# The first 8 MB of a ReLU row sum: even 64 KB stretches in one half of the partitions, odd ones in the other

## The chip, the core and the metric

The kernel runs on one NeuronCore of one Trainium2 chip. The metric is the device time of one execution in microseconds (us). The time before is the median of 3 runs.

## What is computed

The input has 32 x 512 rows of 1024 float32 values, 64 MB in all. Each row is clamped at zero and summed, which leaves one float32 for a row.

```python
batch, seq, dim = 32, 512, 1024
...
def reference(x):
    relu_x = np.maximum(x, 0)
    return np.sum(relu_x, axis=-1).astype(np.float32)
```

## The kernel before

The 16384 rows are seen as 128 partitions of 128 rows. A row of the input is 4 KB, and 16 rows, one column group of a buffer in one partition, are a contiguous 64 KB stretch.

**Two views of memory.** The first 2048 rows (8 MB, `N1`) have a view of their own, `xf`: partition p holds rows 16 p to 16 p + 15, so the 128 stretches of 64 KB lie one behind the other in memory and go to partitions 0, 1, 2 and so on. The remaining 14336 rows are `xv`: partition p holds 112 consecutive rows, and a load takes the same 16 of each partition, so its 64 KB stretches are 448 KB apart. The output has the same two views, `of` and `ov`. `rows(m, n)` and `sums(m, n)` pick the view: below 16 (`ROWS`) the first one.

**Loads.** There are three SBUF buffers `io0` to `io2`, each of 128 x 16 x 1024 float32 (8 MB). All DMAs are issued by SyncE (SP), in program order. Seven loads of 8 MB go round the three buffers (the loop over `j`); they are called load 0 to load 6 here. Load 0 alone takes its rows from `xf`. It is moved ahead of the opening of the program by `open_without_barrier`. Loads 1 and 2 follow with no wait. From load 3 on, a load waits on a semaphore that DVE raises when it has summed the buffer's old content. The last 16 rows of each partition come in six smaller loads: 8 rows, 4 rows, and the last 4 rows in four pieces (`head`, `end`, `middle` and the piece `last`). Each load has a semaphore of its own that stands at 16 when everything has landed.

**Arithmetic.** For the 8 MB buffers ScalarE (ACT) clamps a stretch in place (`clamp`, line 144) and VectorE (DVE) then sums it by rows (`total`, line 152). Loads 0 and 1 are taken whole (16 rows at once), loads 2 to 4 in two halves of 8, load 5 as 7 + 7 rows with two rows left to ACT, and load 6 row by row: 8 rows on ACT (`act_row`, line 159) and 8 on DVE (`dve_row`, line 167), each of which clamps and sums in one instruction. The tail's rows are divided between ACT and DVE in the same manner, and the last pieces are split by column so that all engines end close together. ACT's first instruction is a table load that waits for load 0 (line 142).

**Stores.** The sums gather in `res` (128 x 128). Three stores follow all the loads in SP's queue (line 115): columns 0 to 15 to `of` (8 KB), the next 110 columns to `ov` (55 KB), and the last two (1 KB) when the last sums are there.

Of the kernel before, what the change touches and what calls it, by code (L numbers as in the profile page):

```python
# [7 lines left out]
P = 128  # L8

ROWS = 16  # L10
# [20 lines left out]
def kernel(tc: tile.TileContext, x: bass.AP, out: bass.AP):  # L31
    nc = tc.nc
    sems = Semaphores(tc)

    tc.close()
    tc.compile()
    nc.cur_bb = nc.bb_map[tc.start_bb_name]
    body = nc.cur_bb.bb.instructions
    ends = list(body)
    body.clear()  # L40
    n_stores = relu_sum(nc, sems, x, out)
    body.extend(ends)


    nc.cur_bb = nc.bb_map[tc.start_bb_name + "_end"]
    nc.cur_bb.bb.instructions.clear()
    nums = sorted(s.num for s in (*sems.loads, sems.act, sems.dve))
    cleared = range(nums[0], nums[-1] + 1)
    assert len(cleared) == len(nums)
    nc.sync.sem_clear(cleared)  # L50
    nc.sync.wait_ge(sems.stored, 16 * n_stores).then_inc(sems.stored, -16 * n_stores)
    open_without_barrier(tc, EARLY)
# [12 lines left out]
def relu_sum(nc, sems: Semaphores, x: bass.AP, out: bass.AP):  # L65
    x_flat = x.flatten_outer_dims()
# [8 lines left out]
    res = nc.alloc_sbuf_tensor("res", [P, NT], F32)  # L75
# [4 lines left out]


    N1 = P * ROWS
    xf = x_flat[:N1].rearrange("(p m) d -> p m d", p=P)
    xv = x_flat[N1:].rearrange("(p m) d -> p m d", p=P)
    o_flat = out.rearrange("b s -> (b s)")
    of = o_flat[:N1].rearrange("(p m) -> p m", p=P)
    ov = o_flat[N1:].rearrange("(p m) -> p m", p=P)

    def rows(m, n):
        if m < ROWS:  # L90
            return xf[:, m : m + n, :]
        return xv[:, m - ROWS : m - ROWS + n, :]

    def sums(m, n):
        if m < ROWS:
            return of[:, m : m + n], res[:, m : m + n]
        return ov[:, m - ROWS : m - ROWS + n], res[:, m : m + n]

    n_load = n_act = n_dve = n_store = 0
# [10 lines left out]
    def store(m, n, act, sem, count):  # L110
        nonlocal n_store
        dst, src = sums(m, n)
        if act:
            nc.sync.wait_ge(sems.act, act)
        nc.sync.dma_start(out=dst, in_=src).wait_op(sem, count, "sem-ge").then_inc(
            sems.stored, 16
        )
        n_store += 1
# [63 lines left out]
    m = 0  # L182
    for j in range(NB):
        buf = bufs[j % NBUF]
        loaded = load(buf[:, :, :], rows(m, ROWS), j >= NBUF and freed[j - NBUF])
        c = 0
        act_waits = dve_waits = loaded
        for n in TWO[j]:
            clamp(buf[:, c : c + n, :], act_waits)
            total(buf[:, c : c + n, :], m + c, n)  # L190
            act_waits = None
            c += n
        for _ in range(ACT[j]):
            act_row(buf[:, c, :], res[:, m + c : m + c + 1], act_waits)
            act_waits = None
            c += 1
        for _ in range(DVE[j]):
            dve_row(buf[:, c, :], res[:, m + c : m + c + 1], dve_waits)
            dve_waits = None
            c += 1  # L200
        assert c == ROWS
        freed.append((n_act, n_dve))
        m += ROWS
# [4 lines left out]
    for n in TAIL:  # L208
        loaded = load(
            buf[:, c : c + n, :], rows(m, n), None if c else freed[NB - NBUF]  # L210
        )
        for i in range(n):
            if i % 2 == 0 or (n == 8 and i == 7):
                act_row(buf[:, c, :], res[:, m : m + 1], loaded if i == 0 else None)
            else:
                dve_row(buf[:, c, :], res[:, m : m + 1], loaded if i == 1 else None)
            c += 1
            m += 1

    flat = buf[:, :, :].rearrange("p c d -> p (c d)")  # L220
    src = rows(m, 4).rearrange("p c d -> p (c d)")
    at = c * D
    head = 2 * D + HEAD
# [91 lines left out]
```

## Time and profile before

| what | value |
|---|---|
| time, median of 3 runs | 160.84 us (160.82 to 161.14) |
| span of the profiled execution | 159.7 us, so the median lies 1.1 us above the span |
| DVE busy | 118.8 us, 74% of the span |
| ACT busy | 103.6 us, 65% |
| moved by DMA | 67.18 MB, mean 421 GB/s over the span |
| chain of waits that ended last | DVE 45%, DMA 45%, ACT 9% |
| ACT's wait for load 0 | 22.0 us |

The span is the time from the first to the last instruction of the profiled execution. The page gives shares of that span; the DMA share is the part of 16 DMA engines' time that packets took. A row of one partition, contiguous on both sides, goes as one packet. TensorE is not used. Other lines of the profile are shown where the prediction reads them.

### The profile page before, as it was taken

To read this page: it belongs to the slowest core of one execution; us is meant where nothing else is said; L and a number is where in the kernel's file an instruction comes from. 1 tells how busy PE (TensorE), PEld (TensorE's weight loads), DVE (VectorE), ACT (ScalarE), POOL (GpSimd) and SP (SyncE) were. 2 spreads that over 40 slices of the span, in tenths; PEclk is the share of its full clock that TensorE was granted. 3 is DMA by queue.
4 is the path that set the end of the run, shared out by engine and by line. 5 is a ranking of instruction groups with operands and counts; after the bars stand their busy time and mean duration, and the time that the engine had idled before them with its cause. 6 is when DMAs were issued, how large, how long until landed. Compare 5 with 4: busy or idle time off the path is not lost.

```text
span 159.7 us, 125 instructions
## 1 busy us (share of the span) xinstructions
DVE 118.8 (74%) x44; ACT 103.6 (65%) x53; POOL 1.0 (1%) x5
## 2 busy tenths in 40 slices
DVE  0000000006999799999999999999999799999986
ACT  0000049993699808996099951999329993496995
POOL 0000000000000000000000000000000000000001
DMA  7996996996997997979969969969969969898993
GB/s 263 525 525 263 525 509 279 525 509 279 525 476 312 525 443 345 525 328 460 525 279 509 525 263 525 525 263 525 509 279 525 492 295 525 353 435 386 407 409 128
DMA packets 2304, 67.18 MB, mean 421 GB/s; under 512 B 640, under 2 KB 768, under 8 KB 1024
## 3 DMA queue, kind: packets, MB, share of 16 engines
q1 hardware_dynamic: 2304, 67.18, 98.0%
HBM read 67.11 MB, written 0.07 MB: 421 GB/s over the span
## 4 chain that ended last, share of the span: by engine, by line
DVE 45%; DMA 45%; ACT 9%; SPq 1%; issue 0%
DMA io<-in_x_dram 45%; DVE res L152 43%; ACT io L144 9%; DVE io L167 1%; SPq L103 1%; DVE io L126 1%; DVE io L254 0%
## 5 line engine op out<-in xcount | busy, mean ns | idle before, releaser
L152 DVE TENSOR_REDUCE res<-io 128x8 f32<-128x8192 f32 (+2 forms) x10 | 101.1, 10175 | 38.9 <-ACT io L144 38.9
L144 ACT ACTIVATE io<-io 128x8192 f32<-128x8192 f32 (+2 forms) x10 | 81.8, 8218 | 25.9 <-DMA io<-in_x_dram 25.9
L159 ACT ACTIVATE io<-io 128x1024 f32<-128x1024 f32 x18 | 18.8, 1043 | 6.6 <-DMA io<-in_x_dram 6.6
L167 DVE TENSOR_SCALAR_CACHE_REDUCE io<-io 128x1024 f32<-128x1024 f32 x14 | 16.2, 1214 | 0.5 <-DMA io<-in_x_dram 0.4
L142 ACT ACT_TABLE_LOAD x1 | 1.3, 1283 | 22.0 <-DMA io<-in_x_dram 22.0
L159 ACT ACTIVATION_READ_ACCUMULATOR io<-io 128x1 f32 x18 | 3.4, 187 | 0.0
L234 POOL TENSOR_SCALAR io<-io 128x254 f32<-128x254 f32 x1 | 0.8, 840 | 155.1 <-DMA io<-in_x_dram 155.1
L167 DVE DVE_READ_ACCUMULATOR io<-io 128x1 f32 x14 | 1.1, 82 | 0.0
L126 DVE TENSOR_SCALAR_CACHE_REDUCE io<-io 128x552 f32<-128x552 f32 (+1 forms) x2 | 1.1, 596 | 0.0
L121 ACT ACTIVATE io<-io 128x321 f32<-128x321 f32 (+1 forms) x2 | 0.9, 426 | 0.1
L254 DVE SCALAR_TENSOR_TENSOR io<-last,io 128x254 f32<-128x254 f32 x1 | 0.4, 425 | 0.0
L121 ACT ACTIVATION_READ_ACCUMULATOR io<-io 128x1 f32 x2 | 0.4, 187 | 0.0
L121 ACT ACTIVATE last<-last 128x153 f32<-128x153 f32 x1 | 0.3, 332 | 0.0
L121 ACT ACTIVATION_READ_ACCUMULATOR last<-last 128x1 f32 x1 | 0.2, 187 | 0.0
L126 DVE DVE_READ_ACCUMULATOR io<-io 128x1 f32 x2 | 0.2, 84 | 0.0
L299 POOL MEMSET const-bfloat16-1.0<- 128x1 bf16 x1 | 0.1, 101 | 0.0
L299 POOL MEMSET const-uint8-127<- 128x1 uint8 x1 | 0.1, 101 | 0.0
L299 POOL MEMSET const-float32-0.0<- 128x1 f32 x1 | 0.1, 99 | 0.2 <-issue 0.2
L299 POOL MEMSET const-float32-1.0<- 128x1 f32 x1 | 0.1, 98 | 0.0
L254 DVE DVE_READ_ACCUMULATOR io<-last,io 128x1 f32 x1 | 0.1, 83 | 0.0
## 6 DMA issues: line engine op xcount, KB each, us to landing
io<-in_x_dram SPq DMA_DIRECT2D x1, 4096.0 KB, 23.8
io<-in_x_dram SPq DMA_DIRECT2D x1, 2048.0 KB, 28.3
io<-in_x_dram SPq DMA_DIRECT2D x1, 1151.0 KB, 30.6
io<-in_x_dram SPq DMA_DIRECT2D x1, 436.5 KB, 31.2
io<-in_x_dram SPq DMA_DIRECT2D x1, 259.0 KB, 31.4
last<-in_x_dram SPq DMA_DIRECT2D x1, 201.5 KB, 31.4
io<-in_x_dram SPq DMA_DIRECT2D x7, 29.1
out_dram<-res SPq DMA_DIRECT2D x1, 55.0 KB, 1.6
```

The lines of the kernel that those rows point to most:

```text
L103: dma = nc.sync.dma_start(out=dst, in_=src)
L121: nc.scalar.activation(out=ap, in_=ap, func=RELU, accum_out=accum_out).wait_op(*after, "sem-ge").then_inc(sems.end, 1)
L126: i = nc.vector.tensor_scalar(out=ap, in0=ap, scalar1=0.0, scalar2=None, op0=MAX, op1=ADD, accum_out=accum_out,)
L142: nc.scalar.preload_act_table(RELU).wait_op(loaded, 16, "sem-ge")
L144: i = nc.scalar.activation(out=ap, in_=ap, func=RELU)
L152: nc.vector.tensor_reduce(out=res[:, m : m + n], in_=ap, axis=mybir.AxisListType.X, op=ADD).wait_op(sems.act, n_act, "sem-ge").then_inc(se ...
L159: i = nc.scalar.activation(out=ap, in_=ap, func=RELU, accum_out=accum_out)
L167: i = nc.vector.tensor_scalar(out=ap, in0=ap, scalar1=0.0, scalar2=None, op0=MAX, op1=ADD, accum_out=accum_out,)
L234: nc.gpsimd.tensor_scalar(out=clamped, in0=clamped, scalar1=0.0, scalar2=None, op0=MAX).wait_op(loaded, 16, "sem-ge").then_inc(sems.end, 1)
L254: nc.vector.scalar_tensor_tensor(out=clamped, in0=last[:, : 2 + LAST_DVE], scalar=0.0, in1=clamped, op0=MAX, op1=ADD, accum_out=res[:, NT ...
L299: nc = _bacc.Bacc("TRN2", target_bir_lowering=False, num_devices=1)
```

## The change

The view of the first 8 MB is turned. Memory's 128 stretches of 64 KB are numbered 2 q + h, with q from 0 to 63 and h either 0 or 1. Partition 64 h + q now holds stretch 2 q + h: partitions 0 to 63 hold stretches 0, 2, 4 and so on, and partitions 64 to 127 hold 1, 3, 5 and so on. The DMA's memory side so has the counts 2, 64 and 16384 (float32) in place of 128 rows one behind the other; the SBUF side is `io0` as before. The store of the first 16 columns of `res` gets the same order on the output's side: 2, 64 and 16. Everything else stays.

```diff
     N1 = P * ROWS
-    xf = x_flat[:N1].rearrange("(p m) d -> p m d", p=P)
+    xf = x_flat[:N1].rearrange("(q h m) d -> h q (m d)", h=2, m=ROWS)
     xv = x_flat[N1:].rearrange("(p m) d -> p m d", p=P)
     o_flat = out.rearrange("b s -> (b s)")
-    of = o_flat[:N1].rearrange("(p m) -> p m", p=P)
+    of = o_flat[:N1].rearrange("(q h m) -> h q m", h=2, m=ROWS)
     ov = o_flat[N1:].rearrange("(p m) -> p m", p=P)
 
     def rows(m, n):
         if m < ROWS:
-            return xf[:, m : m + n, :]
+            assert (m, n) == (0, ROWS)
+            return xf
         return xv[:, m - ROWS : m - ROWS + n, :]
 
     def sums(m, n):
         if m < ROWS:
-            return of[:, m : m + n], res[:, m : m + n]
+            return of, res[:, m : m + n]
         return ov[:, m - ROWS : m - ROWS + n], res[:, m : m + n]
```

## The prediction

> **What bounds the kernel now.** I read the page's DMA queue first, because DVE and ACT are busy for only 74% and 65% of the span.
>
> ```profile
> DVE 118.8 (74%) x44; ACT 103.6 (65%) x53; POOL 1.0 (1%) x5
> ...
> DMA packets 2304, 67.18 MB, mean 421 GB/s; under 512 B 640, under 2 KB 768, under 8 KB 1024
> ## 3 DMA queue, kind: packets, MB, share of 16 engines
> q1 hardware_dynamic: 2304, 67.18, 98.0%
> ```
>
> The packets filled 98.0% of 16 engines' time: the input stream is the bound from end to end. The packet count also tells how a DMA is dealt out. There are 13 loads and 3 stores, each of 128 partition rows: 16 x 128 = 2048 packets. The 256 left over are 16 DMAs x 16, one small closing packet for each engine of each DMA. So all 16 DMAs ran on all 16 engines, and each 8 MB load gave an engine 128 / 16 = 8 rows of 64 KB.
>
> Next the rate, by stretches (columns: stretch, length, busy time of DVE, ACT and POOL, clock, DMA share, GB/s; a packet counts where it starts).
>
> ```profile
> 1.00:2.00 1.00, 0.00 (x0) 0.00 (x0) 0.00 (x0) 1.00 2.89 983
> ...
> 10.00:15.00 5.00, 0.00 (x0) 0.00 (x0) 0.00 (x0) 1.00 0.97 419
> ```
>
> The second row holds 419 GB/s x 5 us = 2.1 MB, or 32 rows of 64 KB, in 0.97 x 16 x 5 = 77.6 engine-us: **2.42 us a row on one engine**, 27.1 GB/s each. The first row holds 15 rows in 2.89 x 16 = 46.2 engine-us, 3.08 us each: the opening wave costs 0.66 us more per engine than a steady row, once.
>
> The timeline (start, length, engine, line, operation) gives the spacing of loads and the start.
>
> ```profile
> 0.00 1.33 SPq L103 DMA_DIRECT2D io<-in_x_dram  x3
> ...
> 21.99 1.28 ACT L142 ACT_TABLE_LOAD   x1 [21.99 <-DMA io<-in_x_dram]
> ```
>
> ```profile
> 99.38 13.95 ACT L144 ACTIVATE io<-io 128x8192 f32<-128x8192 f32 x2 [5.40 <-DMA io<-in_x_dram]
> ...
> 118.73 12.24 ACT L144 ACTIVATE io<-io 128x7168 f32<-128x7168 f32 x2 [5.40 <-DMA io<-in_x_dram]
> ```
>
> Three loads are issued in the first 1.33 us; the first has landed at 21.99, and later ones land 118.73 - 99.38 = 19.35 us apart, which is 8 x 2.42. From the first landing to the end of the span there are 159.7 - 22.0 = 137.7 us. The span is 159.7 us and the median of the runs 160.84: 1.1 us lie outside the span, and I add them at the end.
>
> The groups by shape give what must happen between a landing and the next use of its buffer (busy, mean ns).
>
> ```profile
> L152 DVE TENSOR_REDUCE res<-io 128x8 f32<-128x8192 f32 x6 | 51.6, 8679 | 0.0
> ...
> L152 DVE TENSOR_REDUCE res<-io 128x16 f32<-128x16384 f32 x2 | 34.4, 17222 | 38.0 <-ACT io L144 38.0
> L144 ACT ACTIVATE io<-io 128x16384 f32<-128x16384 f32 x2 | 27.7, 13856 | 4.2 <-DMA io<-in_x_dram 4.2
> ```
>
> **The change, part by part.** Bytes, buffers, compute instructions, waits and the order of SP's queue stay. Two DMAs of 16 get another memory side: the first load and the 8 KB store.
>
> *How the first load is dealt out.* This decides everything. Before, both sides of the copy have an outermost count of 128, and the packet count shows 16 equal shares of 8. After, the SBUF side still counts 128 outermost, but the memory side counts 2 (even and odd), then 64, then 64 KB runs. The two halves can't be merged into one step: memory goes 128 KB from row to row and back again for the second half. If a copy is cut along the outermost count of both sides, in equal parts, only two parts exist: 64 rows for one engine and 64 for another. If it is cut by the SBUF rows alone, 16 shares of 8 remain. No DMA in this trace has an outermost count other than 128, so the trace bounds this from both sides only: 8 rows per engine as now, or 64. I take 64, because equal parts of one step on either side is the only form that all 16 DMAs of the trace have. [...]
>
> *Price of the first load.* 64 rows x 2.42 = 154.8 us, plus 1.0 us from issue to the first packet (no packet starts in the stretch before 1 us) and something between last packet and landing: at most 21.99 - 1.0 - 3.08 - 7 x 2.42 = 1.0 us, part of which is that the sixteen engines start up to 1 us apart, so I take 0.3: 156.1 us instead of 22.0. With only two engines on it, I count the opening row at the steady rate.
>
> *What else runs meanwhile.* Loads 1 and 2 are issued at once and still go to 16 engines. Fourteen of them finish their 16 rows at about 1.5 + 16 x 2.42 = 40 us, then idle. The two engines of load 0 reach their own 8 + 8 rows only behind its 64. While the fourteen run, one of the two engines at a time writes partition rows that belong to the share of one of the others. Here is an unknown cost. If 27.1 GB/s is the limit of an engine, they don't meet: 0 us. If it is the limit of the way into a group of partitions, two engines on the same rows share it half and half; for the 38.7 us of the other engine's 16 rows ours goes at half speed and loses 19.4 us. It can't cost less than nothing, for the steady row is the fastest of the trace. The trace's one crowded row is the opening wave, 3.08 against 2.42: engines do hold each other up, and the steady rows, all equal at 2.42 with separate partition rows, were never tested on shared ones. I take 19.4, for engines on separate partitions all stopping at the same 2.42 looks more like a way in at its limit, and keep 0 as the other end. [...]
>
> So load 0 lands at 156.1 + 19.4 = 175.5 us.
>
> *What follows.* The two engines then carry what they carried before: 8 rows of each later load and their share of the last pieces, without a pause if SP issues each load before they run dry. SP's loads wait for DVE to free a buffer, so I check this. Load 0: table load 1.3, ACT 13.9, DVE 17.2, buffer free at 175.5 + 32.4 = 207.9. The two engines have load 2 to move until 175.5 + 2 x 19.35 = 214.2: load 3 is queued with 6.3 us to spare, against 1.0 to 2.0 us from issue to packets at the start. Load 1 lands at 194.8, ACT is done at 208.7, DVE at 225.9; the engines are busy until 233.5: 7.6 us to spare. Load 2 takes DVE 2 x 8.7, free at 243.3 against 252.9. The margin then grows by 2 us a load, as DVE's 17.4 is under 19.35. So these waits are hidden by the queue of the two engines; were a margin gone, its shortfall would be added once. The tail's loads and its ACT and DVE rows find the same spacing as before, so 137.7 us follow the first landing.
>
> *The 8 KB store.* 128 packets of 64 B, 64 on each of two engines rather than 8 on each of 16. It is the last but two in SP's queue, behind all loads. Two bounds: no more than now, or 8 times now. Its cover is the closing arithmetic, the last store's issue and that store's own flight (issue to landing 1.4 us). I count 0; if its cover were gone, some tenths.
>
> *Sum.* 175.5 + 137.7 = 313.2 us of span, + 1.1 = **314.3 us**. Without sharing 156.1 + 137.7 + 1.1 = 294.9 us.
>
> **The rivals.**
> 1. *Two engines, no sharing*: 294.9 us. For it: an engine that moves one row after another at a constant 2.42 may be its own limit. Against: the reading above.
> 2. *All 16 engines still serve the load* (the cut follows SBUF rows; this is the side that ends not slower). Then each engine has 8 rows, and only the addresses of the opening wave change: rows that start together lie in neighbouring stretches rather than megabytes apart. The opening wave's 0.66 us is all that can be saved, at most 160.84 - 0.66 = 160.2 us; if it stays, 160.8; if engine pairs collide more, as much again, 161.5. For it: SBUF's side is untouched. It decides if the count of closing packets stays 256. The point from which it turns to slower is an opening row over 3.08 us.
> 3. *Two engines, and they come off worse than half* while the other fourteen run, or a later load comes late: over 320 us, up to 294.9 + 38.7 = 333.6 if they wait for the other engine's 16 rows altogether.
>
> **How the numbers follow.** Two engines with sharing 0.54 (314.3), two without 0.26 (294.9), two and worse 0.04, sixteen 0.16. The last divides into faster 0.08, unchanged 0.04 and slower 0.04; 0.2% of the time, 0.3 us, is about what a measurement of this kernel can tell from no change. So faster 0.08, same 0.04, slower 0.54 + 0.26 + 0.04 + 0.04 = 0.88. The range runs over the first two cases: from 290 (no sharing, with 5 us for engines that move a row slightly faster when alone) to 320 (sharing, with 6 us, the smallest buffer margin lost). It holds 0.80. All of it is of one sign.
>
> **What would show it.** Packets 16 x 128 + 14 x 16 + 2 x 2 = 2276 instead of 2304, and under 512 B 612 instead of 640. ACT's first wait for the DMA 175 us (156 without sharing) instead of 22.0. The DMA strip near full until about 40 us, then about 1 to 2 tenths of 16 engines (2 / 16 = 0.12, 54 GB/s) until some 208 us, then patches of full rate with gaps. DVE's and ACT's busy time unchanged. A page with 2304 packets and a first landing near 22 would make the prediction wrong at its first step; 2276 packets and a landing near 156, at the sharing.

## The result and the profile after

The changed kernel takes **327.6 us** (327.47 to 327.64) against 160.91 us before, a ratio of 2.035 with a 95% interval of 2.032 to 2.037. The forecast was 314.3 us, from 290 to 320: the direction, the two engines and the sharing of partitions were forecast, but the price of the sharing was not, and the forecast was 13.3 us short, outside its range.

On the page after, the busy times of DVE and ACT are those of before, and the packet counts are the ones the forecast named, to the packet. The third line is the DMA busy share in 40 slices of 8.2 us each.

```profile
DVE 118.7 (36%) x44; ACT 103.5 (32%) x53; POOL 1.0 (0%) x5
...
DMA  9969898911111111111111111109999999998993
...
DMA packets 2276, 67.18 MB, mean 206 GB/s; under 512 B 612, under 2 KB 740, under 8 KB 996
...
q1 hardware_dynamic: 2276, 67.18, 54.9%
```

2276 is 2048 rows and 14 x 16 + 2 x 2 closing packets: load 0 and the 8 KB store ran on two engines each. The DMA strip shows one tenth of sixteen engines, that is two engines, for most of the first 219 us, where it was full throughout before.

The windows (stretch, length, DVE, ACT, POOL, clock, DMA share, GB/s) cut the first part in three.

```profile
5.00:20.00 15.00, 0.00 (x0) 0.00 (x0) 0.00 (x0) 1.00 1.06 433
40.00:60.00 20.00, 0.00 (x0) 0.00 (x0) 0.00 (x0) 1.00 1.01 210
100.00:120.00 20.00, 0.00 (x0) 0.00 (x0) 0.00 (x0) 1.00 0.13 56
```

From 5 to 20 us sixteen engines move 433 GB/s: load 1 beside load 0. The trace has a time for every packet: of the 99 rows that started in this window 92 took 2.4 to 2.6 us and six took 4.8, so that two engines held each other up and the others went on as before. From 100 to 120 us two engines are left, at 56 GB/s or 2.4 us a row. The middle row is the one that the forecast didn't have: all sixteen are busy (1.01) and move 210 GB/s, 64 rows in 323 engine-us, **5.05 us a row**. That is load 2 beside load 0. No engine is spared: each of the 96 rows that started between 30 and 60 us took 4.8 to 5.1 us.

The waits, and SP's queue in the timeline:

```profile
ACT L143 <- DMA io<-in_x_dram: 188.6, 1, 188.6
```

```profile
0.00 26.56 SPq L104 DMA_DIRECT2D io<-in_x_dram  x3
...
221.02 18.36 SPq L104 DMA_DIRECT2D io<-in_x_dram  x2
```

Load 0 lands at 188.6 us (22.0 before; 175.5 forecast). From there to the end of the span are 326.3 - 188.6 = 137.7 us, the same as before and as forecast: nothing was lost or won after the first landing. The first three issues, 1.33 us before, now take 26.56: one of them, the third, took 25.3. So 13.1 of the 13.3 us of the miss lie in the landing of load 0 (188.6 - 175.5), and the experiments go there.

### The profile page after: what moved, and what is told of

Same layout as the page of the kernel before. It is cut to its first block, busy times and chain, and to the rows that moved or that the text cites. A ratio compares the mean times of both kernels' runs of the same rounds, so it can differ in the third digit from the quotient of the medians.

```text
span 326.3 us, 125 instructions
## 1 busy us (share of the span) xinstructions
DVE 118.7 (36%) x44; ACT 103.5 (32%) x53; POOL 1.0 (0%) x5
## 2 busy tenths in 40 slices
DMA packets 2276, 67.18 MB, mean 206 GB/s; under 512 B 612, under 2 KB 740, under 8 KB 996
## 3 DMA queue, kind: packets, MB, share of 16 engines
q1 hardware_dynamic: 2276, 67.18, 54.9%
## 4 chain that ended last, share of the span: by engine, by line
another core or an unknown queue 59%; DVE 22%; DMA 9%; ACT 9%; SPq 0%; issue 0%
DVE res L153 21%; DMA io<-in_x_dram 9%; ACT io L145 8%; ACT L143 0%; DVE io L168 0%; DVE io L127 0%; SPq L104 0%; DVE io L255 0%
## 5 line engine op out<-in xcount | busy, mean ns | idle before, releaser
L143 ACT ACT_TABLE_LOAD x1 | 1.3, 1283 | 188.6 <-DMA io<-in_x_dram 188.6
## 6 DMA issues: line engine op xcount, KB each, us to landing
io<-in_x_dram SPq DMA_DIRECT2D x1, 259.0 KB, 31.3
```

Of the source, the lines that this page charges most:

```text
L143: nc.scalar.preload_act_table(RELU).wait_op(loaded, 16, "sem-ge")
```

## The experiments

Each ran once beside the kernel before, which took 160.9 to 161.0 us, except where a ratio is given. "First engine" and "second engine" are the two that carry load 0: partitions 0 to 63 and 64 to 127 by the view's outermost index; the trace names no partitions.

**Nothing beside load 0.** Load 1 waits for load 0's semaphore, and load 2 stands behind it.

```diff
+        if n_load in HOLD:      # HOLD = (1,)
+            dma.wait_op(sems.loads[0], 16, "sem-ge")
```

> Loads 1 and 2 are issued only when load 0 has landed; all else is as in the changed kernel. Theory (two engines for load 0, 2.42 us a row when nothing runs beside them): load 0 lands at 156.1 us, the next two loads start with an opening wave of their own (2.6 us), then the known 137.7 us and 1.2 us outside the span: about 297.6 us, 30 us faster than the changed kernel. Rival (load 0's two engines are slow in themselves, by the spread of the addresses): load 0 lands at 188 us again and the time stays over 327 us.

Measured: 299.0 us. Windows and waits:

```profile
1.00:2.00 1.00, 0.00 (x0) 0.00 (x0) 0.00 (x0) 1.00 0.42 131
...
20.00:40.00 20.00, 0.00 (x0) 0.00 (x0) 0.00 (x0) 1.00 0.12 52
```

```profile
ACT L146 <- DMA io<-in_x_dram: 157.3, 1, 157.3
```

The price of the two engines alone is right to 1.2 us (157.3 against 156.1). About 1 us of this is the opening row: the first window holds two rows in 0.42 x 16 = 6.7 engine-us, 3.4 us each. So the opening row is slow with only two engines at work too, and not because sixteen crowd each other. From then on they move a row in 2.4 us. So 31.3 of load 0's 188.6 us are paid for company.

**Only load 2 held.** The same edit with `HOLD = (2,)`: load 1 runs beside load 0.

> Only load 2 (the third) waits until load 0 has landed; load 1 runs beside load 0. Theory of shared partition rows: only the engine that writes the same partitions as one of load 1's engines is held up, 4 of its rows at double time: load 0 lands at 156.1 + 9.7 = about 166 us and the time is about 305 us. Theory that the third load runs at half rate because of its own addresses: load 0 lands at 166 us too, but load 2 takes about 41 us instead of 19 after that, and the time is about 325 us. Rival that any load beside load 0 halves all engines: load 0 lands near 176 us, time about 315 us.

Measured: 306.6 us.

```profile
ACT L146 <- DMA io<-in_x_dram: 167.5, 1, 167.5
```

```profile
170.00:185.00 15.00, 2.33 (x1) 12.63 (x1) 0.00 (x0) 1.00 0.97 419
```

Load 1's company costs 167.5 - 157.3 = 10.2 us (9.7 expected), and load 2, alone with the later loads, is not slow: from 170 us on it moves at 419 GB/s. So its addresses alone don't make it slow, and load 1 beside load 0 doesn't halve all engines. The other 21 us are due to load 2 standing beside load 0.

**Exchanged rows.** Loads 1 and 2 take each other's rows.

```diff
+        m = {1: 2, 2: 1}.get(j, j) * ROWS
```

> Loads 1 and 2 exchange their rows (the sums go to the same places as before); order, buffers and waits stay. If the half rate of all engines between 26 and 66 us comes from the addresses that load 2 reads, it moves with them: rows take about 5.1 us in the first 40 us and 2.42 us in the load after. If it comes from the place of the load in the queue (issued 25 us late, when the others have run dry), nothing moves: 2.42 us rows for the second load, 5.1 us for the third, time 327.6 us.

Measured: 327.85 us, and the half rate stayed where it was: 424 GB/s from 5 to 20 us and 210 from 40 to 60. So it isn't the memory addresses that load 2 reads.

**Load 2 issued late, and a queue filled on purpose.** SP's 25 us with the third issue were the next suspect. One kernel issues load 2 at 33 us, past the 26.56 us at which SP had the third issue behind it in the changed kernel; the other is meant to fill the queues of the kernel before.

```diff
+    nc.vector.memset(idle[:, :], 0.0).then_inc(sems.tick, 1)
+    for i in range(TICKS):      # 14; each waits for the memset and adds 1
+        nc.vector.tensor_reduce(out=ticks[:, i : i + 1], in_=idle[:, :], ...)
...
+        if n_load == 2:
+            dma.wait_op(sems.tick, 1 + TICKS, "sem-ge")
```

> The changed kernel, but load 2 is issued about 33 us late, behind 14 sums over a cleared scratch tile on the idle DVE, when the two engines' queues have room again; it still runs beside load 0. Theory that SP's held-up issue is what puts load 2 at half rate on all engines: now only the engines that share partitions with load 0's two move at half rate, the others at 2.42 us a row; load 0 lands at about 177 us, time about 316 us. Rival that any 16-engine load started late beside load 0 goes at half rate: all rows at about 5 us again, load 0 lands at about 187 us, time about 327 us.

Measured: 327.9 us, load 0 landing at 188.6, and the half rate again:

```profile
40.00:60.00 20.00, 0.00 (x0) 0.00 (x0) 0.00 (x0) 1.00 1.02 210
```

No single issue of a load took over 0.71 us here. The theory of the held-up issue falls.

```diff
+        if j == 2:
+            for f in range(8):
+                nc.sync.dma_start(out=small[:, 2 * f : 2 * f + 2], in_=xf[:, f, 0:2])
```

> The kernel before (all loads on 16 engines), with 8 small loads of 8 bytes a partition put between loads 1 and 2 to fill every engine's queue, so that SP is held up when it issues load 2; nothing reads them. Theory that a held-up issue gives half rate, with no load on two engines at all: load 2's rows take about 5 us, its landing comes about 20 us late, time about 181 us. Rival (half rate comes from the company of load 0 on two engines, not from the hold-up): rows stay at 2.42 us, time 160.9 to 162 us.

Measured: 162.05 us. The timeline shows that SP was indeed held up (start, length):

```profile
0.90 32.57 SPq L189 DMA_DIRECT2D small<-in_x_dram  x8
...
33.52 4.86 SPq L106 DMA_DIRECT2D io<-in_x_dram  x1
```

and load 2's window is at full rate all the same:

```profile
45.00:60.00 15.00, 14.11 (x2) 10.18 (x1) 0.00 (x0) 1.00 0.97 419
```

SP stood for over 30 us in its own issuing instructions, but what it issued afterwards wasn't slower. That the queues were full is inferred from this stand. The 1.1 us over the kernel before include a second opening wave behind the eight small loads: load 2's first rows took 2.6 to 3.2 us.

**Which partitions load 0 is at.** In the changed kernel's trace the rows of load 0's two engines can be followed, for each row starts within 0.02 us of the end of the one before. From 5 to 20 us, at full rate, one engine moved its rows 3 to 8 in 2.42 us each and the other its rows 2 to 4 in 4.84 us each: one of the two had a partner. From 30 to 65 us, at half rate, they were at rows 12 to 18 and 8 to 14. The one ahead is taken for the first engine. That load 2 would be spared beside the first engine's rows 32 to 39 was the author's estimate; no run before this one shows why it should be. The next two kernels test whether the place counts: the late issue with 35 sums instead of 14 puts load 2 beside these rows, and the other moves load 1 to the place where load 2 was slow.

> As the run with 14 sums, but with 35: load 2 starts at about 80 us, when load 0's first engine is at its 32nd row of 64 and the second some 4 rows behind. [...] Theory that a load started late, from idle engines, is always at half rate beside load 0: rows at 5.1 us, load 2 takes 41 us, load 0 lands near 188 us, time 327 to 328 us.

Measured: 317.1 us. By the theory of the late start it would be 327 to 328; load 0 with one partner at a time, eight of its rows at double time, gives an estimate of 157.3 + 19.4 + 137.7 + 1.3 = 315.7 us.

```profile
84.00:97.00 13.00, 0.00 (x0) 0.00 (x0) 0.00 (x0) 1.00 0.94 383
```

```profile
ACT L147 <- DMA io<-in_x_dram: 178.0, 1, 178.0
```

Load 2 beside load 0, late, from idle engines, and at 383 GB/s instead of 210. Of the 76 rows that started in this window 71 took 2.4 to 2.5 us and five 3.9 to 4.9, which is less than two engines' time in 13 us. From the run with 14 sums this one differs in the time of the issue alone, and so in the rows at which load 0 stands: 383 GB/s beside these rows, 210 beside the earlier ones.

```diff
-        if n_load == 2:         # 14 sums again
+        if n_load == 1:
```

> Loads 1 and 2 are both issued at about 33 us, load 1 first. Theory that the rows of load 0 at the time decide: load 1, which went at full rate when it started at 1 us, now goes at half rate too, and load 2 behind it as far as it falls beside rows 8 to 31 of the first engine; load 0 lands later than 188 us, up to 198, time up to 338 us. Theory that the third load alone is slow, whatever the time: load 1's rows at 2.42 us, load 2's at 5.1, load 0 lands at about 188 us, time about 328 us.

Measured: 337.8 us (up to 338 expected).

```profile
60.00:80.00 20.00, 0.00 (x0) 0.00 (x0) 0.00 (x0) 1.00 1.01 210
80.00:100.00 20.00, 0.00 (x0) 0.00 (x0) 0.00 (x0) 1.00 1.00 210
```

```profile
ACT L147 <- DMA io<-in_x_dram: 198.6, 1, 198.6
```

Load 1 is slow here too, and load 2 behind it; both together now cost 41.3 us (198.6 - 157.3). The third load isn't special, nor is a late start as such: where load 0 stands at the time decides. Its place in memory moves along with its partitions, and these two runs don't part them; what speaks for the partitions is the first window of the next run.

**One engine instead of two.** The kernel before with its first 8 MB as three loads, the last of them 61 partitions on a single engine.

```diff
+            for lo, hi in ((64, 128), (61, 64), (0, 61)):
+                nc.sync.dma_start(out=buf[lo:hi, :, :], in_=xf[lo:hi, :, :])
```

> The kernel before, with the first 8 MB in plain order but as three loads: partitions 64 to 127 (16 engines), 61 to 63 (3 engines), then 0 to 60, a count that no number from 2 to 16 divides, so one engine with 61 rows. Loads 1 and 2 follow on 16 engines. Only this one engine now writes into other engines' partitions. Theory that all engines fall to half rate only when two such engines hold up others at the same time: beside the 61 rows, load 1 and load 2 run near 400 GB/s in total, only one engine at a time is at half rate; load 0 lands near 185 us, time about 324 us. Rival that one such engine is enough: load 2, from about 45 us on, runs at about 210 GB/s with rows of 5 us, load 0 lands near 193 us or later, time 331 us or more.

Measured: 337.65 us, and 2308 packets: 2048 + 15 x 16 + 16 + 3 + 1, the single engine among them.

```profile
5.00:20.00 15.00, 0.00 (x0) 0.00 (x0) 0.00 (x0) 1.00 1.02 210
...
46.00:62.00 16.00, 0.00 (x0) 0.00 (x0) 0.00 (x0) 1.00 1.04 418
62.00:78.00 16.00, 0.00 (x0) 0.00 (x0) 0.00 (x0) 1.00 0.43 160
```

By the time alone the rival would have won, and that reading would be wrong: the rate beside the single engine is 418 GB/s, not 210. Of the 102 rows that started from 46 to 62 us 95 took 2.4 to 2.6 us and six 4.7 to 4.9, three of these on the single engine. The time is long because my sum for this kernel was poor. The 61 rows start only at 30.4 us: the 16-engine piece took 5.1 us a row until 21 us, and then every engine had one row of 8.5 to 9.2 us. 30.4 + 61 x 2.42 + 1.0 for a slow opening row + 8 rows at double time (19.4) = 198.4, and load 0 landed at 198.6. So the single engine held up one other engine at a time: six rows of 4.7 to 4.9 us are 1.8 engines' time in the 16 us. Load 2's half rate, with all sixteen at 5 us a row, appeared only beside a load on two engines. That it takes two held-up pairs at once is the author's estimate: where every row is slow, the trace doesn't tell pairs apart.

This trace shows two things more. The first window is 64 partitions in plain memory order, on sixteen engines, and it has the half rate too: it goes with the partitions and not with an interleaved memory side. And the rows of 8.5 to 9.2 us came on all sixteen engines although the piece that ran then, partitions 61 to 63, was on three of them and the others had begun load 1. So a load on two engines isn't the only company in which all sixteen were slow; how large a crowd must be wasn't measured.

**Sixteen engines and the same interleave.** Two ways to mix the stretches without the two-engine load: 16 interleaved groups (`h=16` in both views), and two loads of 64 partitions each.

> The view of the first 8 MB with 16 interleaved groups instead of 2: partition 8 h + q holds stretch 16 q + h, the memory side counts 16, 8, 16384. If the number of engines follows the outermost count of both sides, 16 engines get 8 rows each: 2304 packets, 640 under 512 B. If then nothing is shared: the time before, 160.8 us within 0.7. If the cut into 16 consecutive groups puts two engines on the same way into partitions: 8 rows at 4.84 us, first landing about 41 us, time about 180 us. If the outermost count is not what decides: any other packet count.

Measured: 182.3 us, 2304 packets, first landing 43.3 us.

```profile
20.00:40.00 20.00, 0.00 (x0) 0.00 (x0) 0.00 (x0) 1.00 1.01 210
```

```diff
+            for h in range(2):
+                nc.sync.dma_start(out=buf[64 * h : 64 * h + 64, :, :], in_=xf[h])
```

> The changed order of the first 8 MB, but moved as two loads of 64 partitions each (even stretches, then odd), and stored as two stores: 64 rows on both sides, so 16 engines with 4 rows of each half. Theory of shared ways into the partitions: 64 partitions have half as many ways as 128, two engines on each: rows at about 5 us, first landing about 42 us, time about 181 us. Rival (an engine's own 2.42 us is the limit): first landing 22 us, time about 161 us.

Measured: 182.4 us, first landing 43.3 us, 210 GB/s from 5 to 40 us. In both, all sixteen engines are busy (DMA share 1.01 and 1.02) and the rows take 5.1 us: an outermost count of 16 or 64 brought all engines to work, but not to their full rate. Of the forms tried, only the plain order with 128 on both sides kept 2.42 us a row on sixteen engines. That the shares are eight consecutive partitions in the one and four in the other was the author's estimate and is not shown; the trace doesn't name partitions.

**Four groups.** `h=4` in both views, loads 1 and 2 held.

> Four interleaved groups instead of two (the memory side counts 4, 32, 16384), with loads 1 and 2 held until load 0 has landed. Number of engines by the outermost count: 4, with 32 rows each, 2290 - 10 = 2280 packets. Theory of shared ways into partitions (the engine of partitions 0 to 31 and that of 32 to 63 go through the same ways in step, and so do the other two): rows at 4.84 us, load 0 lands at about 157 us and the time is about 299 us, the same as with two engines. Rival (engines don't hold each other up): rows at 2.42 us, load 0 lands at about 80 us, time about 222 us.

Measured: 300.3 us, 2280 packets, load 0 at 158.7.

```profile
20.00:60.00 40.00, 0.00 (x0) 0.00 (x0) 0.00 (x0) 1.00 0.25 52
```

Twice as many engines (share 0.25 instead of 0.12) move the same 52 GB/s. 32 rows in 0.25 x 16 x 40 = 160 engine-us are 5.0 us a row. This is what the theory of pairs on the same ways gives; the rival's 2.42 us a row is out.

**The store alone.** The kernel before with only the store's new order.

> The kernel before with only the 8 KB store in the new order (so these sums land in other rows than they belong to); the load stays. Two of 16 engines for 128 packets of 64 bytes: 2290 packets instead of 2304 and no change of time that can be told apart, 160.9 us within 0.3. Rival that the store's end comes late: some tenths of a us more, up to 161.6.

Measured in 3 rounds: 160.98 us against 160.98, ratio 1.0004 (0.9994 to 1.0014), 2290 packets. The store costs nothing, as counted.

No variant beat the kernel before.

## Why the prediction had the direction right and the size wrong

- **How the load is dealt out**: right. 2 engines for a count of 2, 4 for 4, 16 for 16, 1 for 61, each seen in the closing packets (2276, 2280, 2304 and 2308 in all).
- **Price of the first load**: 156.1 forecast, 157.3 measured with nothing beside it, 1.2 us short, about 1 of it the opening row, which I had counted at the steady rate (64 x 2.42 is 154.9, too, not 154.8).
- **Sharing or not**: I took sharing, rightly. The rival of 294.9 us fell with the row of 5.0 us in the run with four groups and with the 10.2 us of load 1. One of my two reasons was wrong: I read the opening wave's 3.08 us as engines that hold each other up, but the opening row takes 3.4 us with two engines alone.
- **Price of sharing: the step that failed.** The prediction had "for the 38.7 us of the other engine's 16 rows ours goes at half speed and loses 19.4 us". Measured, the term is 31.3 us (188.6 - 157.3). For two loads where only one partner at a time is held up, 19.4 is nearly right: the late run with 35 sums has 178.0 - 157.3 = 20.7 us. What the prediction had at nothing is an effect on all engines at once. In the changed kernel, load 2 comes beside rows 12 to 18 of one of load 0's engines and 8 to 14 of the other. Then all sixteen fall to 5.05 us a row, load 2's rows last 41 us instead of 20, and load 0's engines stay at half speed twice as long: 188.6 - 178.0 = 10.6 us more.
- **Sum of the miss**: 1.2 for the first load alone, 1.3 for the sharing, 10.6 for the halving of all, 0.2 outside the span (1.3 for 1.1): 13.3 us.
- **What follows** and **the buffers**: right. Later loads come 19.35 us apart, load 3 is issued at 221.0, and the two engines run dry of load 2 at about 227: the 6.3 us of margin were there.
- **The third rival** ("come off worse than half") had a chance of 0.04 and held the outcome between 320 and 333.6 us. Its reason was another one (a partner that goes first), but its weight was too small: I had one mechanism for contention, no trace of it, and gave its spread 5 us on one side and 6 on the other.

The runs show load 2 at 210 GB/s on all sixteen engines beside some rows of load 0, and at 383 GB/s beside others; why the fourteen that have no part in load 0 are slowed is open.

## What to carry to other kernels

Before changing the order of a DMA's view, look at the outermost count on both sides: in these runs it set how many engines worked (2 for a count of 2, 4 for 4, 16 for 16, 64 and 128, 1 for 61), and the closing packets of the page (one per engine and DMA) tell it at once: 2276 packets instead of 2304 here. Then ask which partitions each engine gets, for sixteen engines moved 419 GB/s in the plain order with 128 on both sides, and 210 with sixteen interleaved groups or with a load of 64 partitions, about eight times the 27.1 of one engine (217). And the load on few engines wasn't a local cost: it delayed every later load on those engines (load 1 landed at 207.9 us, 41.3 before), and beside some of its rows it halved the others (210 GB/s from 40 to 60 us, 433 from 5 to 20).

## What the runs showed that I had not expected

- Beside a load on two engines all sixteen went at 210 GB/s (5.05 us a row) at one place of that load and at 383 to 433 GB/s at others; a load on one engine left the total at 418 GB/s. While three engines ran the piece at partitions 61 to 63, all sixteen had a row of 8.5 to 9.2 us.
- Where a single pair was held up, each got half, 4.8 us a row against 2 x 2.42 = 4.84; where four or all sixteen were, it was a little less than half, 5.0 to 5.1 us.
- With 64 rows waiting on two engines, SP was held up for 25 us at the third issue; with eight small loads ahead, for over 30. It cost little by itself: 1.1 us at most in the run with the small loads.
